# GpSimd's instruction order in the first pass of branch B, written by hand

## The chip, the cores and the metric

The kernel runs on one core of a Trainium2 chip. The core has a matrix engine (TensorE, PE in the views, with PEld for its weight loads), VectorE (DVE), ScalarE (ACT), GpSimd (POOL) and SyncE (SP), which here only issues DMAs. Each engine takes its instructions strictly in the order in which they stand in its stream, and semaphores hold an instruction until what it needs is there. The metric is the device time of one execution in microseconds (us), lower is better.

## The reference

One encoder block over 1024 tokens and 16 meta tokens, width 1024. Cut to what matters here:

```python
h = concat(meta, x)                       # 1040 x 1024
proj = rms_norm(h) @ w_in                 # qa ka va | qb kb vb | ga gb
y_a = differential_attention(qa, ka, va)  # branch A: 4 heads, two softmaxes each, all keys
y_b = windowed_gqa(qb, kb, vb, sink)      # branch B: 8 heads in 2 groups, band of 3 blocks + meta
merged = sigmoid(ga) * (y_a @ w_ba) + sigmoid(gb) * (y_b @ w_bb)
h = h + merged @ w_o
h = h + swiglu(rms_norm(h), w_gate, w_up, w_down)
out = rms_norm(h)[16:]

# branch B, for a block of 128 queries
p = exp(s - m)                            # s: scores + bias, m: their maximum and the sink's
denom = sum(p) + exp(sink - m)
y = (p / denom) @ v
```

Matrix products are done with operands split in a high and a low part (high = the value rounded to the matrix engine's fp32r format, low = the rest), so that one product is three: high x high, high x low, low x high.

## The kernel before

**Stages.** The normed input is transposed into `hT_hi` and `hT_lo`. The first projections (kb, and the queries of group 0 of branch B) run while it is still being transposed. Then comes the stretch of the program that the change touches: `attend_b` for the first two tiles of branch B, the projection vb (`project_v(C_VB, ...)`, L503), the other six tiles of group 0 (`units_b(0, qb, first_b)`, L646), the projections qa, va, ka of branch A's heads 0 and 1 (`project_a(0)`, `project_a(1)`), and, in four chunks, the token sums (`token_sums(c)`, L510). After it come the queries of group 1 (`project_qb(1, qb)`), the tiles of group 1 together with heads 2 and 3, then branch A's attention with the gates, the merge, and the feed-forward layer. The token sums are differences and sums of quarters of `hT` for products in Strassen's manner; they are stored in `ts_d` and read again only by `load_sums`, first at L706, after all projections.

**One tile of branch B** (`attend_b`, L316): for each of 4 heads two matmuls make scores in a PSUM bank (`bps`, L331, two banks), VectorE adds the bias and takes the running minimum of the negated scores into the SBUF tile `bs` (L333, two buffers), ScalarE takes exp with the row sum (L337), VectorE adds the sink's term and takes the reciprocal (`bdn`, L340 and L341), GpSimd scales the four heads' rows by it (L343) and copies the meta columns into `bmd` (L347). `finish` transposes each block on TensorE (`bpt`, L356, two PSUM banks), ScalarE writes the high part and VectorE the low part (`btr`, L358 and L360), TensorE multiplies with `vb` (`bpy`, L362, one bank), and `by` goes to DRAM. A middle tile has four blocks, an end tile three.

**One projection** is three chunks of tokens (two for qa and qb) by 8 weight blocks by 3 terms, L214. `prep` (L174) loads a weight tile `w_c`, ScalarE writes its high part `wh_c` and GpSimd (for most) the low part `wl_c` by a subtraction (`split`, L118). The third of the three terms needs `wl_c`. The names carry the weight's column: c2176 is vb, c0 / c1024 / c512 are qa, va, ka of head 0, c128 / c1152 / c640 those of head 1.

**One chunk of token sums** is 11 additions or subtractions of 128x512 on GpSimd into `ta` tiles (three buffers), four of whose results `keep` splits on ScalarE and VectorE into `to` (two buffers) and stores.

**What sets the order.** Up to branch A's attention a scheduler orders the instructions of every engine: it simulates the program on a timeline and takes what is ready there, so that the program's text is only a preference. GpSimd alone is ordered by hand (`tc.manual_schedule(engines={Pool})`: as the text has it) from L682 on, just ahead of the queries of group 1. TensorE is ordered by hand from branch A's attention on.

Of the kernel before, what the change touches and what calls it, by code (L numbers as in the profile page):

```python
# [73 lines left out]
def encoder_block(ctx: ExitStack, tc: tile.TileContext, x, meta, norm_mix, w_in, lq1, lk1, lq2, lk2,  # L74
# [7 lines left out]
    def f32(ap):  # L82
        return ap.bitcast(F32)
# [32 lines left out]
    def split(hi, lo, src, lo_eng):  # L116
        nc.scalar.activation(hi, src, AF.Copy)  # L117
        lo_eng.tensor_tensor(lo, src, f32(hi), ALU.subtract)  # L118
# [55 lines left out]
    def prep(col, name, p=None, lo_eng=None):  # L174
        w = wpool.tile([P, DC, P], F32, tag="w", name=f"w_{name}", bufs=2)
        if isinstance(col, tuple):
            for i, k in enumerate(col):
                nc.sync.dma_start(w[:, 4 * i:4 * i + 4], g_weights(k, 1, 0, P))
        else:
            nc.sync.dma_start(w, w_in[:, col:col + P].rearrange("(c p) n -> p c n", p=P))  # L180
        if p:
            both = p.tile([P, 2, DC, P], F32R, tag="k0", name=f"wb_{name}", bufs=1)
            wh, wl = both[:, 0], both[:, 1]
        else:
            wh = wpool.tile([P, DC, P], F32R, tag="wh", name=f"wh_{name}", bufs=W_BUFS)
            wl = wpool.tile([P, DC, P], F32R, tag="wl", name=f"wl_{name}", bufs=W_BUFS)
        split(wh, wl, w, lo_eng or nc.gpsimd)
        return wh, wl
# [11 lines left out]
    def ensure(n):  # L200
        while order and len(prepped) < n:
            col = order.pop(0)
            prepped[col] = prep(col, f"c{col[0] if isinstance(col, tuple) else col}", lo_eng=nc.vector if col in on_vector else None)
# [3 lines left out]
    def project_steps(col, chunks, name, evac):  # L207
        wh, wl = prepped.pop(col)
        terms = [(wh, hT_hi), (wh, hT_lo), (wl, hT_hi)]
        for at, n in chunks:  # L210
            ps = pp_bank(f"pp_{name}_{at}")
            for c in range(DC):
                for i, (a, b) in enumerate(terms):
                    nc.tensor.matmul(ps[:, :n], a[:, c, :], b[:, c, at:at + n],  # L214
                                     start=(c == 0 and i == 0), stop=(c == DC - 1 and i == 2))
                if c == DC - 1:
                    evac(ps[:, :n], at, n)
                yield

    def project(col, chunks, name, evac):  # L220
        ensure(1)
        for i, _ in enumerate(project_steps(col, chunks, name, evac)):
            if i % DC == V_AT and turning_v:
                next(turning_v[0], None)
        ensure(W_BUFS - 1)

    def evac_split(scale, consume):
        def run(ps, at, n):
            st = stage.tile([P, 2, 512], F32R, tag="qk", name="qk_stage", bufs=QK_BUFS)
            hi, lo = st[:, 0, :n], st[:, 1, :n]  # L230
            if scale is None:
                nc.scalar.activation(hi, ps, AF.Copy)
                nc.vector.tensor_tensor(lo, ps, f32(hi), ALU.subtract)
            else:
                nc.scalar.activation(hi, ps, AF.Copy, scale=scale)
                nc.vector.scalar_tensor_tensor(lo, ps, scale, f32(hi), ALU.mult, ALU.subtract)
            consume(f32(st), at, n)
        return run

    def project_v(col, name, evac):  # L240
        vt = vtpool.tile([P, L + NM], F32, tag="vt", name=f"vt_{name}", bufs=1)
        project(col, K_CHUNKS, name, lambda ps, at, n: nc.scalar.copy(vt[:, at:at + n], ps))
        nc.vector.tensor_copy(vt[:, L:L + NM], vt[:, S:L])

        def turn():
            for b in range(3):
                nb = 4 if b < 2 else 1
                kp = P if b < 2 else 2 * NM
                pt = pp_bank(f"pv_{name}_{b}").rearrange("p (c t) -> p c t", c=4)
                for i in range(nb):  # L250
                    k = 4 * b + i
                    nc.tensor.transpose(pt[:kp, i, :], vt[:, k * P:k * P + kp], ident)
                evac(pt[:kp, :nb, :], 4 * b, nb, kp)
                yield

        turning_v[:] = [turn()]
# [39 lines left out]
    def new_qb(g):  # L296
        return bpool.tile([P, 4, S], F32R, tag="qb", name=f"qb{g}", bufs=1)
# [73 lines left out]
    qb = new_qb(0)  # L371
# [127 lines left out]
    nc.vector.tensor_scalar(neglam, lam_s[:, 1:2], lam_s[:, 0:1], LAMBDA_INIT, ALU.subtract, ALU.subtract)  # L499


    first_b = [attend_b(0, t, qb) for t in range(2)]
    project_v(C_VB, "vb", vb_evac)  # L503
    flush_v()
    def quad(hl, kh, half):
        return (hT_hi, hT_lo)[hl][:, 4 * kh:4 * kh + 4, half * 512:half * 512 + 512]
# [3 lines left out]
    def token_sums(c):  # L510
        tt = nc.gpsimd.tensor_tensor

        def new(name):
            return tpool.tile([P, 512], F32, tag="ta", name=f"ta{name}_{c}", bufs=3)

        def part(hl, kh, half):
            return f32(quad(hl, kh, half)[:, c])

        def keep(p, src):
            to = tpool.tile([P, 2, 512], F32R, tag="to", name=f"to{p}_{c}", bufs=2)  # L520
            split(to[:, 0], to[:, 1], src, nc.vector)
            nc.sync.dma_start(ts_d[p][:, :, c, :], f32(to))

        t1, low = new(1), new("l1")
        tt(t1, part(0, 0, 1), part(0, 0, 0), ALU.subtract)
        tt(low, part(1, 0, 1), part(1, 0, 0), ALU.subtract)
        tt(t1, t1, low, ALU.add)
        keep(5, t1)
        t3, t2 = new(3), new(2)
        tt(t3, part(0, 1, 1), part(0, 0, 1), ALU.subtract)  # L530
        tt(t2, part(1, 1, 1), part(1, 0, 1), ALU.subtract)
        tt(t3, t3, t2, ALU.add)
        keep(7, t3)
        tt(t2, t3, part(0, 0, 0), ALU.add)
        tt(t2, t2, part(1, 0, 0), ALU.add)
        keep(6, t2)
        t4 = new(4)
        tt(t4, part(0, 1, 0), t2, ALU.subtract)
        tt(t4, t4, part(1, 1, 0), ALU.add)
        keep(4, t4)  # L540

    def project_a(h):
        def q_consume(st, at, n):
            for m in range(2):
                nc.sync.dma_start(qa_d[h][m, :, at:at + n].rearrange("(a d) t -> d a t", a=2),
                                  st[64 * m:64 * m + 64, :, :n])

        def k_consume(st, at, n):
            for m in range(2):
                nc.sync.dma_start(ka_d[h][m, :, at:at + n].rearrange("(a d) t -> d a t", a=2),  # L550
                                  st[64 * m:64 * m + 64, :, :n])

        def va_evac(pt, k0, nb, kp):
            vs = stage.tile([P, 2, 4, P], F32R, tag="qk", name="va_stage", bufs=QK_BUFS)
            hi, lo = vs[:kp, 0, :nb, :], vs[:kp, 1, :nb, :]
            nc.scalar.activation(hi, pt, AF.Copy)
            nc.vector.tensor_tensor(lo, pt, f32(hi), ALU.subtract)
            nc.sync.dma_start(va_d[h][:kp, :, k0:k0 + nb, :], f32(vs)[:kp, :, :nb, :])

        project(C_QA + h * P, Q_CHUNKS, f"qa{h}", evac_split(-(2.0 ** (2 * h - 1)), q_consume))  # L560
        project_v(C_VA + h * P, f"va{h}", va_evac)
        project(C_KA + h * P, K_CHUNKS if h < AH - 1 else K_CHUNKS[::-1], f"ka{h}", evac_split(None, k_consume))

    def units_b(g, qb, pending=(), extra=lambda t: None):
        pending = list(pending)
        for t in range(len(pending), NT):
            if len(pending) > 1:
                pending.pop(0)()
            pending.append(attend_b(g, t, qb))
            extra(t)  # L570
            if len(pending) > 1:
                pending.pop(0)()
        for p in pending:
            p()
# [68 lines left out]
                what(g_done[i])  # L643
                g_done[i] += 1

    units_b(0, qb, first_b)  # L646
    for c in range(2):
        token_sums(c)
    project_a(0)
    token_sums(2)  # L650
    project_a(1)
    token_sums(3)

    def load_k(h, m, k):
        nc.sync.dma_start(f32(k)[:, 0, :], ka_d[h][m])
# [23 lines left out]
        nc.sync.dma_start(f32(v)[2 * NM:3 * NM, 0, 8, :], va_d[h][:NM, 1, 8, :])  # L679
        return v  # L680

    order_pool = tc.manual_schedule(engines={mybir.EngineType.Pool})  # L682
    order_pool.__enter__()
    qb = new_qb(1)
    project_qb(1, qb)
    for n in range(2):
# [210 lines left out]
    for n in range(AH * NT + T_LAG):  # L897
        scoring, turning = iter(()), iter(())
        if n < AH * NT:
            h, t = divmod(n, NT)  # L900
# [548 lines left out]
    for n in range(nf, len(steps)):  # L1449
# [4 lines left out]
        if p in LOADS:  # L1454
            at, half, col = LOADS[p]
            if at <= j < at + 4:
                t, cols = 4 * half + j - at, slice(col * 512, col * 512 + 512)
# [60 lines left out]
```

## Time and profile before

| | us |
|---|---|
| median of 3 runs | 1446.95 (1446.73 to 1448.22) |
| the profiled execution | 1446.43 |
| its span, first to last instruction | 1444.6 |

| engine | busy us | share of the span | instructions |
|---|---|---|---|
| TensorE matmuls | 1423.5 | 99% | 7279 |
| TensorE weight loads | 1221.1 | 85% | 7279 |
| VectorE | 901.6 | 62% | 1624 |
| ScalarE | 679.5 | 47% | 1290 |
| GpSimd | 642.6 | 44% | 605 |

The profile is one execution. Matmuls are pipelined: a record lasts until its end, which is modelled, and the next one starts earlier. So what a matmul costs in a dense stream is the step from one start to the next, and "busy" does not mean that TensorE ran at its peak. Times in the views are counted from the span's start. Of the 1444.6 us, the stretch that the change touches lies between about 35 us (the first token sum on GpSimd in the kernel before) and 200 us (the first score of group 1).

### The profile page before, as it was taken

The page shows a single profiled execution, that of the slowest core. Times are in us where ns is not written, and L with a number is a line of the kernel's source. Part 1 is how long each engine was busy: PE and PEld are TensorE (multiplying, and loading weights), DVE is VectorE, ACT ScalarE, POOL GpSimd, SP SyncE. Part 2 cuts the span into 40 slices and gives each one's busy share as a digit, 9 for nine tenths or more (in the row PEclk, how much of TensorE's full clock was granted, in tenths as well). Part 3 has the DMA queues.
Part 4 walks back from the last instruction along what each step waited for, and adds up shares of the span by engine and source line. Part 5 has one row for each costly group of instructions (what it writes and reads, how often), then busy time and mean ns, then how long its engine had stood idle before and what let it go on. Part 6 is the DMA issues. An engine that isn't in the chain of part 4 may idle for free.

```text
span 1444.6 us, 21159 instructions
## 1 busy us (share of the span) xinstructions
PE 1423.5 (99%) x7279; PEld 1221.1 (85%) x7279; DVE 901.6 (62%) x1624; ACT 679.5 (47%) x1290; POOL 642.6 (44%) x605
## 2 busy tenths in 40 slices
PE   8999999999999999999999999999999999999997
PEld 6988989988898989888888878888888888888886
DVE  7478536637697989624614966554555553787567
ACT  6356535545665656545413643333333333444454
POOL 5589227743333333334522665544544552000444
PEclk9999999999999999999999999999999999999999
DMA  8367668995558473586602534333332333964343
GB/s 245 87 211 231 195 160 271 283 289 208 189 168 258 147 226 126 190 255 204 224 32 88 152 103 162 110 102 110 101 103 96 110 102 102 334 205 140 124 130 139
DMA packets 188891, 242.41 MB, mean 168 GB/s; under 512 B 18208, under 2 KB 115936, under 8 KB 188784
## 3 DMA queue, kind: packets, MB, share of 16 engines
q1 hardware_dynamic: 188784, 241.07, 52.5%
q8 instruction: 57, 0.93, 0.3%
q14 instruction: 50, 0.41, 0.1%
HBM read 157.45 MB, written 77.00 MB: 162 GB/s over the span
## 4 chain that ended last, share of the span: by engine, by line
PE 80%; POOL 6%; DVE 5%; issue 4%; DMA 3%; ACT 2%; SPq 0%; POOLq 0%; DVEq 0%; ACTq 0%
PE pg L1299 27%; PE pd L1393 9%; PE pg L742 7%; PE ppa L786 6%; PE po L1076 6%; PE aps L802 3%; PE pp_qb L214 3%; PE apy L841 3%; POOL oa L118 3%; PE pp_ka L214 2%; PE pp_va L214 2%; PE apt L828 2%; PE pp_qa L214 2%; PE bpt L356 1%; PE bpy L362 1%
## 5 line engine op out<-in xcount | busy, mean ns | idle before, releaser
L118 POOL TENSOR_TENSOR wop<-wf,wop 128x512 fp32r<-128x512 f32 x128 | 173.5, 1360 | 164.7 <-ACT wop L117 150.3
L1299 PE MATMUL pg<-t,wop 128*128 128x512 f32 x1056 | 242.6, 389 | 0.0
L1299 PEld LDWEIGHTS pg<-t,wop 128*128 128x128 f32 x1056 | 198.2, 188 | 41.2
L1393 PE MATMUL pd<-ob,oa 128*128 128x512 f32 x924 | 209.9, 389 | 0.4 <-POOL oa L118 0.4
L1393 PEld LDWEIGHTS pd<-ob,oa 128*128 128x128 f32 x924 | 173.3, 188 | 36.8 <-POOL oa L118 0.9
L1299 PE MATMUL pg<-b,wop 128*128 128x512 f32 x792 | 185.6, 392 | 2.3 <-DVE c L1308 2.3
L1299 PEld LDWEIGHTS pg<-b,wop 128*128 128x128 f32 x792 | 149.4, 189 | 34.2 <-issue 2.4
L742 PE MATMUL pg<-hT_hi,gop 128*128 128x512 f32 x384 | 142.9, 397 | 0.0
L118 POOL TENSOR_TENSOR oa<-ra,oa 128x512 fp32r<-128x512 f32 x33 | 44.1, 1337 | 170.0 <-ACT oa L117 168.6
L117 ACT ACTIVATE wop<-wf 128x512 fp32r<-128x512 f32 x128 | 80.2, 631 | 83.3 <-PE pg L1299 47.8
L118 POOL TENSOR_TENSOR gop<-gr,gop 128x512 fp32r<-128x512 f32 x47 | 62.0, 1321 | 105.9 <-ACT gop L117 105.9
L117 ACT ACTIVATE oa<-ra 128x512 fp32r<-128x512 f32 x77 | 48.7, 632 | 106.1 <-PE pd L1393 46.0
L810 ACT ACTIVATE as<-as,amn 128x1040 f32<-128x1040 f32 x64 | 74.5, 1165 | 47.3 <-DVE amn L805 43.2
L1134 DVE TENSOR_TENSOR s<-wf,wf 128x512 f32<-128x512 f32 x22 | 23.7, 1077 | 107.6 <-DMA wf<-in_w_ff_gate_dram 57.4
L802 PE MATMUL aps<-ak,aq 128*128 128x392 f32 (+1 forms) x384 | 90.1, 330 | 0.7 <-DVE amn L805 0.4
L1076 PE MATMUL po<-woh,mT 128*128 128x512 f32 x384 | 88.1, 390 | 0.0
L1076 PEld LDWEIGHTS po<-woh,mT 128*128 128x128 f32 x384 | 71.9, 188 | 14.8
L742 PEld LDWEIGHTS pg<-hT_hi,gop 128*128 128x128 f32 x384 | 72.7, 189 | 11.3 <-DVE gk L747 0.2
L802 PEld LDWEIGHTS aps<-ak,aq 128*128 128x128 f32 x384 | 69.6, 189 | 14.3 <-DVE amn L805 2.0
L343 POOL TENSOR_SCALAR bs<-bs,bdn 128x432 f32<-128x432 f32 (+1 forms) x64 | 41.1, 662 | 87.1 <-DVE bdn L341 74.3
L742 PE MATMUL pg<-hT_lo,gop 128*128 128x512 f32 x192 | 76.1, 396 | 0.0
L813 POOL TENSOR_SCALAR as<-as,adn,neglam 128x1040 f32<-128x1040 f32 x32 | 39.1, 1220 | 63.9 <-DVE adn L811 44.6
(289 smaller groups left out, 3105.9 us busy)
## 6 DMA issues: line engine op xcount, KB each, us to landing
ra<-aop SPq DMA_DIRECT2D x77, 256.0 KB, 2.7
wf<-in_w_ff_gate_dram SPq DMA_DIRECT2D x24, 512.0 KB, 3.8
wf<-in_w_ff_up_dram SPq DMA_DIRECT2D x24, 512.0 KB, 3.9
aop<-as SPq DMA_DIRECT2D x44, 256.0 KB, 2.1
w_c<-in_w_in_dram SPq DMA_DIRECT2D x17, 512.0 KB, 6.1
aop<-c SPq DMA_DIRECT2D x33, 256.0 KB, 2.0
ts_d<-to SPq DMA_DIRECT2D x16, 512.0 KB, 3.4
gw<-in_w_in_dram SPq DMA_DIRECT2D x32, 256.0 KB, 4.2
```

Of the source, the lines that this page charges most:

```text
L117: nc.scalar.activation(hi, src, AF.Copy)
L118: lo_eng.tensor_tensor(lo, src, f32(hi), ALU.subtract)
L214: nc.tensor.matmul(ps[:, :n], a[:, c, :], b[:, c, at:at + n], start=(c == 0 and i == 0), stop=(c == DC - 1 and i == 2))
L343: nc.gpsimd.tensor_scalar(st[:, r, :W], st[:, r, :W], dn[:, r:r + 1], 1.0, ALU.mult, ALU.mult)
L742: nc.tensor.matmul(ps, op[:, a, c], quad(b, *act)[:, c], start=(p in (2, 5, 1) and c == 0 and i == 0), stop=(p in (2, 3, 4) and c == 3 and ...
L786: nc.tensor.matmul(ps, w[:, a, j, :], src(j, b, tk), start=(j == 0 and n == 0), stop=(j == 3 and n == 2))
L802: nc.tensor.matmul(ps[:, :n], qs[m][:, t * P:(t + 1) * P], ks[m][:, vv, k0:k0 + n], start=(vv == 0), stop=(vv == 1))
L810: nc.scalar.activation(s[m][:, 0:L], s[m][:, 0:L], AF.Exp, bias=low, scale=-1.0, accum_out=dn[:, m:m + 1])
L841: nc.tensor.matmul(py[:, cols], v[:kp, a, k, :], at_[:kp, k, b, :], start=(k == 0 and j == 0), stop=(k == 8))
L1076: nc.tensor.matmul(ps, mT[:, c, a, t * P:(t + 1) * P], wos[q, c][:, b], start=(c == 0 and n == 0), stop=(c == DC - 1 and n == 2))
L1299: nc.tensor.matmul(ps, op[:, x, c, :], b[:, y, c, :], start=(p in (1, 2, 5) and c == 0 and n == 0), stop=(p in (4, 2, 3) and c == 3 and n ...
L1393: nc.tensor.matmul(ps[u], oa[:, a, u * P:(u + 1) * P], ob[:, b, :], start=(p in (1, 2, 5) and j == 0 and k == 0), stop=(p in (2, 3, 4) and ...
```

## The change

```diff
@@ project
                 next(turning_v[0], None)
         ensure(W_BUFS - 1)
+        step_sums(6)
+
+    summing = []
+
+    def step_sums(n):
+        while n > 0 and summing:
+            n -= 1
+            if next(summing[0], True):
+                summing.pop(0)
@@ ahead of branch B's first tile
+    order_pool = tc.manual_schedule(engines={mybir.EngineType.Pool})
+    order_pool.__enter__()
     first_b = [attend_b(0, t, qb) for t in range(2)]
     project_v(C_VB, "vb", vb_evac)
@@ token_sums: a yield behind each of the 11 operations
         tt(t1, part(0, 0, 1), part(0, 0, 0), ALU.subtract)
+        yield
         tt(low, part(1, 0, 1), part(1, 0, 0), ALU.subtract)
+        yield
...
@@ the order of the stages
-    units_b(0, qb, first_b)
-    for c in range(2):
-        token_sums(c)
+    summing += [token_sums(c) for c in range(4)]
+    units_b(0, qb, first_b, lambda t: step_sums(2))
     project_a(0)
-    token_sums(2)
     project_a(1)
-    token_sums(3)
+    step_sums(100)
@@ ahead of group 1
-    order_pool = tc.manual_schedule(engines={mybir.EngineType.Pool})
-    order_pool.__enter__()
     qb = new_qb(1)
```

GpSimd's order by hand now begins ahead of branch B's first tile. In it stand the scalings of the tiles, two token sums behind each of the tiles 2 to 7, and six behind each projection of heads 0 and 1. No operation is added or taken away. The other engines are still ordered by the scheduler, which now sees GpSimd's order as given; their streams differ from the kernel before up to the queries of group 1 and are the same, instruction for instruction, behind them.

GpSimd, from the last token sums of chunk 0 in the kernel before. `ta` are token sums, `wl_c2176` the low part of vb's weight, `bs_0_0` tile 0 of group 0:

```order
L539 TENSOR_TENSOR ta4_0_1607<-ta4_0_1607,hT_lo_134 128x512
L118 TENSOR_TENSOR wl_c2176_938<-w_c2176_935,wh_c2176_937 128x1024
L118 TENSOR_TENSOR wl_c0_1022<-w_c0_1019,wh_c0_1021 128x1024
L343 TENSOR_SCALAR bs_0_0_868<-bs_0_0_868,bdn_0_0_870 128x288 x4
L347 COPY bmd0_150<-bs_0_0_868 128x4x32
L526 TENSOR_TENSOR tal1_1_1615<-hT_lo_134 128x512
L343 TENSOR_SCALAR bs_0_1_901<-bs_0_1_901,bdn_0_1_903 128x432 x4
```

and in the changed kernel, from the same place of the program (behind the last of the input norms):

```order
L352 TENSOR_SCALAR bs_0_0_870<-bs_0_0_870,bdn_0_0_872 128x288 x4
L356 COPY bmd0_150<-bs_0_0_870 128x4x32
L352 TENSOR_SCALAR bs_0_1_903<-bs_0_1_903,bdn_0_1_905 128x432 x4
L356 COPY bmd1_151<-bs_0_1_903 128x4x32
L118 TENSOR_TENSOR wl_c2176_940<-w_c2176_937,wh_c2176_939 128x1024
L118 TENSOR_TENSOR wl_c0_1024<-w_c0_1021,wh_c0_1023 128x1024
L352 TENSOR_SCALAR bs_0_2_1089<-bs_0_2_1089,bdn_0_2_1091 128x432 x4
L356 COPY bmd0_150<-bs_0_2_1089 128x4x32
L536 TENSOR_TENSOR ta1_0_1122<-hT_hi_133 128x512
```

The two weight splits stood ahead of the first scaling and now stand behind the second; chunk 0 of the sums, which stood ahead of both, now begins behind the third.

TensorE at branch B's first tile before (`pp_vb` is the projection vb, `bps_0_0` the scores of tile 0):

```order
L214 MATMUL pp_vb_384_967<-hT_hi_133,wl_c2176_938 128x384
L214 MATMUL pp_vb_384_967<-hT_hi_133,wh_c2176_937 128x384
L214 MATMUL pp_vb_384_967<-hT_lo_134,wh_c2176_937 128x384
L214 MATMUL pp_vb_384_967<-hT_hi_133,wl_c2176_938 128x384
L331 MATMUL bps_0_0_0_872<-kb0_146,qb0_156 128x288
L331 MATMUL bps_0_0_1_876<-kb0_146,qb0_156 128x288
L214 MATMUL pp_vb_384_967<-hT_hi_133,wh_c2176_937 128x384
```

and in the changed kernel:

```order
L340 MATMUL bps_0_2_3_1105<-kb0_146,qb0_156 128x432 x2
L365 MATMUL bpt_0_0_8_1076<-ident_109,bmd0_150 128x128 x4
L365 MATMUL bpt_0_1_0_1127<-ident_109,bs_0_1_903 128x128 x2
L340 MATMUL bps_0_3_0_1174<-kb0_146,qb0_156 128x432 x2
L365 MATMUL bpt_0_1_0_1127<-ident_109,bs_0_1_903 128x128
L340 MATMUL bps_0_3_1_1178<-kb0_146,qb0_156 128x432 x2
L365 MATMUL bpt_0_1_0_1127<-ident_109,bs_0_1_903 128x128
L365 MATMUL bpt_0_1_1_1137<-ident_109,bs_0_1_903 128x128 x4
L365 MATMUL bpt_0_1_2_1147<-ident_109,bs_0_1_903 128x128 x4
L214 MATMUL pp_vb_0_943<-hT_hi_133,wl_c2176_940 128x384
```

Only the first six of vb's 72 matmuls (two terms of each of its three chunks) stood ahead of the scores of tile 0; the other 66 moved behind the scores and transposes of tiles 0 and 1 and scores of tiles 2 and 3.

TensorE among the later tiles before (`pp_ka0` is ka of head 0):

```order
L331 MATMUL bps_0_4_2_1253<-kb0_146,qb0_156 128x432 x2
L214 MATMUL pp_ka0_0_1797<-hT_hi_133,wl_c512_1793 128x384
L214 MATMUL pp_ka0_0_1797<-hT_hi_133,wh_c512_1792 128x384
L331 MATMUL bps_0_4_3_1257<-kb0_146,qb0_156 128x432 x2
L214 MATMUL pp_ka0_0_1797<-hT_lo_134,wh_c512_1792 128x384
L214 MATMUL pp_ka0_0_1797<-hT_hi_133,wl_c512_1793 128x384
L214 MATMUL pp_ka0_384_1836<-hT_hi_133,wh_c512_1792 128x384
L362 MATMUL bpy_0_2_1197<-btr_0_2_1_1203,vb0_148 128x512 x2
```

and in the changed kernel (`pp_va0` is va of head 0):

```order
L340 MATMUL bps_0_4_2_1267<-kb0_146,qb0_156 128x432 x2
L340 MATMUL bps_0_4_3_1271<-kb0_146,qb0_156 128x432 x2
L371 MATMUL bpy_0_2_1211<-btr_0_2_3_1237,vb0_148 128x512
L365 MATMUL bpt_0_3_2_1291<-ident_109,bs_0_3_1170 128x128 x4
L214 MATMUL pp_va0_768_1754<-hT_hi_133,wh_c1024_1681 128x272
L214 MATMUL pp_va0_768_1754<-hT_lo_134,wh_c1024_1681 128x272
L340 MATMUL bps_0_5_0_1338<-kb0_146,qb0_156 128x432 x2
L340 MATMUL bps_0_5_1_1342<-kb0_146,qb0_156 128x432 x2
L371 MATMUL bpy_0_2_1211<-btr_0_2_8_1247,vb0_148 128x512
L365 MATMUL bpt_0_3_3_1301<-ident_109,bs_0_3_1170 128x128 x4
```

Before, matmuls of projections stand between the tiles' own. Now these two of va are the last projection matmuls until tile 7's transposes: the third term of va needs `wl_c1024`, which in GpSimd's new order stands behind the scaling of tile 7 and one token sum. From there on ka, qa, va, ka of heads 0 and 1 and the queries of group 1 follow with no tile among them.

More of the change, by code (lines that the diff above doesn't have):

```diff
@@ L525, in token_sums @@
         tt(t1, part(0, 0, 1), part(0, 0, 0), ALU.subtract)
+        yield
         tt(low, part(1, 0, 1), part(1, 0, 0), ALU.subtract)
+        yield
         tt(t1, t1, low, ALU.add)
+        yield
         keep(5, t1)
@@ L530, in token_sums @@
         tt(t3, part(0, 1, 1), part(0, 0, 1), ALU.subtract)
+        yield
         tt(t2, part(1, 1, 1), part(1, 0, 1), ALU.subtract)
+        yield
         tt(t3, t3, t2, ALU.add)
+        yield
         keep(7, t3)
         tt(t2, t3, part(0, 0, 0), ALU.add)
+        yield
         tt(t2, t2, part(1, 0, 0), ALU.add)
+        yield
         keep(6, t2)
@@ L538, in token_sums @@
         tt(t4, part(0, 1, 0), t2, ALU.subtract)
+        yield
         tt(t4, t4, part(1, 1, 0), ALU.add)
+        yield
         keep(4, t4)
```

## The prediction

> **What bounds the kernel now.** I read the page's engine table first, then busy time by window, then TensorE's timeline.
>
> ```profile
> span 1444.6 us, 21159 instructions
> PE 1423.5 (99%) x7279; PEld 1221.1 (85%) x7279; DVE 901.6 (62%) x1624; ACT 679.5 (47%) x1290; POOL 642.6 (44%) x605
> ...
> core 0: us, PE busy (x) PEld busy (x) DVE busy (x) ACT busy (x) POOL busy (x), PEclk, DMA share, GB/s
> 56.04:200.53 144.49, 142.69 (x819) 128.85 (x818) 84.89 (x172) 72.80 (x168) 76.87 (x76) 1.00 0.67 193
> ```
>
> TensorE is the bound everywhere, and in the stretch that the change touches (from vb's first matmul to group 1's first score) it lacks only 144.49 - 142.69 = 1.8 us of being always busy. A GpSimd order can win little here; it can lose what it makes TensorE wait. Since "busy" hides short stalls, I price TensorE's work by steps from one start to the next:
>
> ```profile
> 56.04 0.34 PE L214 MATMUL pp_vb<-hT_hi,wh_c 128*128 128x384 f32 x1
> 56.22 0.34 PE L214 MATMUL pp_vb<-hT_lo,wh_c 128*128 128x384 f32 x1
> ...
> 63.39 0.43 PE L331 MATMUL bps<-kb,qb 128*128 128x288 f32 x2
> 63.65 0.34 PE L214 MATMUL pp_vb<-hT_hi,wh_c 128*128 128x384 f32 x1
> ...
> 65.22 0.29 PE L214 MATMUL pp_vb<-hT_hi,wl_c 128*128 128x272 f32 x1
> 65.34 0.29 PE L214 MATMUL pp_vb<-hT_hi,wh_c 128*128 128x272 f32 x1
> ...
> 73.26 0.40 PE L214 MATMUL pp_qa<-hT_hi,wh_c 128*128 128x512 f32 x1
> 73.49 0.40 PE L214 MATMUL pp_qa<-hT_lo,wh_c 128*128 128x512 f32 x1
> ...
> 89.70 0.55 PE L331 MATMUL bps<-kb,qb 128*128 128x432 f32 x2
> 90.09 0.34 PE L214 MATMUL pp_va<-hT_hi,wh_c 128*128 128x384 f32 x1
> ...
> 92.41 1.04 PE L356 MATMUL bpt<-ident,bs 128*128 128x128 f32 x8
> 93.20 0.42 PE L214 MATMUL pp_va<-hT_hi,wh_c 128*128 128x384 f32 x1
> ...
> 200.37 0.69 PE L331 MATMUL bps<-kb,qb 128*128 128x288 f32 x4
> ```
>
> A matmul of 384 columns takes 0.175 us, 512: 0.23 (512/384 x 0.175 = 0.233), 272: 0.12, 432: 0.39/2 = 0.195, 288: 0.26/2 = 0.13, a transpose 0.79/8 = 0.10. The same instructions lie between 56.04 and 200.37 in both kernels, 144.3 us, and the streams behind are equal, so what this stretch gains or loses is the whole result.
>
> **The change, part by part. First gap: vb waits for two scalings.** Before, vb covered tile 0's latency. Now TensorE runs 6 of vb's matmuls and stands before tile 0's scores, which need keys that SP's queue is still sending:
>
> ```profile
> 60.01 0.61 SPq L285 DMA_DIRECT2D kb<-qk_stage  x1
> ...
> DMA to landing us min/median/max: 2.0/2.1/3.8
> ```
>
> This is the last issue for group 0; it lands at 60.01 + 2.1 = 62.1. The queue holds the same DMAs in the same order, so nothing comes sooner. The chain behind it:
>
> ```profile
> 65.03 0.52 DVE L333 CUSTOM_DVE_ANT_0 bs<-bps,tbx,nsink 128x288 f32<-128x288 f32 x1 [7.28 <-PE bps L331]
> ...
> 82.36 1.29 POOL L527 TENSOR_TENSOR ta<-ta,tal 128x512 f32<-128x512 f32 x1
> 83.62 2.40 POOL L118 TENSOR_TENSOR wl_c<-w_c,wh_c 128x1024 fp32r<-128x1024 f32 x1
> ...
> 90.79 2.45 POOL L343 TENSOR_SCALAR bs<-bs,bdn 128x432 f32<-128x432 f32 x4 [1.56 <-ACT btr L358]
> ...
> 156.32 0.08 DVE L333 DVE_READ_ACCUMULATOR2_ANT bmn<- 128x1 f32 x1
> ...
> 157.84 1.96 POOL L343 TENSOR_SCALAR bs<-bs,bdn 128x288 f32<-128x288 f32 x4 [5.85 <-ACT btr L358]
> 159.87 0.29 POOL L347 COPY bmd<-bs 128x128 f32<-128x128 f32 x1
> ```
>
> From 62.1: score and hand-over 0.6, four minima of 0.55: 64.9. From a tile's last minimum to its scaling 157.84 - 156.40 = 1.44, and 0.7 for minima of tile 1 that stand between: 67.0. Scaling 1.96 and transposes 0.4: 69.4. In VectorE's new stream two minima of tile 2 stand ahead of tile 1's reciprocal and need the buffer that these transposes free: two of 0.73 (minimum plus its read, rows below), reciprocal and hand-over 0.3: 71.2. Tile 1's scaling 2.45, copy 0.29, `wl_c2176` 2.40, hand-over 0.2: vb's third matmul term starts at 76.5. TensorE's work till then: 6 of vb 0.9, scores 8 x 0.13 + 20 x 0.195 = 4.9, 24 transposes 2.4, together 8.3 of 20.5 us. **12 us idle.**
>
> **Middle, dense.** Rest of vb 10.3 (44 x 0.175 + 22 x 0.12), its transposes 0.9, 8 scores 1.6, qa 48 x 0.233 = 11.2, 20 transposes 2.0, 17 `bpy` 4.0, four of va 0.7, about 1.0 for vb's eviction: 31.6, to 108.1.
>
> **Second gap: tiles 4 to 7 alone.** Until `wl_c1024`, behind tile 7's scaling, only 2 projection matmuls remain. The tiles then go at their own period. VectorE carries most per tile:
>
> ```profile
> L118 DVE TENSOR_TENSOR to<-ta,to 128x512 fp32r<-128x512 f32 x10 | 11.2, 1121 | 7.4 <-ACT to L117 7.2
> L333 DVE CUSTOM_DVE_ANT_0 bs<-bps,tbx,nsink 128x432 f32<-128x432 f32 x14 | 8.7, 656 | 0.9 <-PE bpt L356 0.9
> L360 DVE TENSOR_TENSOR btr<-bpt,btr 128x512 fp32r<-128x512 f32 x13 | 8.4, 673 | 0.0
> L340 DVE TENSOR_TENSOR bdn<-bdn,bes 128x4 f32<-128x4 f32 x5 | 4.8, 968 | 0.9 <-ACT bes L339 0.9
> L335 DVE TENSOR_TENSOR bes<-bmn,sinkb 128x4 f32<-128x4 f32 x5 | 3.5, 707 | 0.1
> L366 DVE TENSOR_TENSOR by<-bpy,by 64x512 f32<-64x512 f32 x4 | 2.7, 674 | 1.2 <-ACT by L365 1.2
> L333 DVE DVE_READ_ACCUMULATOR2_ANT bmn<- 128x1 f32 x18 | 1.4, 78 | 0.0
> ```
>
> Four minima 4 x 0.734 = 2.9, four low parts 2.7, `by` 0.7: 6.3. The two four-column operations and one `to` add 2.8 at these means, 9.1 in all; but 0.7 to 1.0 us for four columns is mostly waiting, beside five or six sums and a split per tile on GpSimd, where now two sums stand. Half of the 2.8 gives 7.7; 0.5 for hand-overs: **8.2 us per tile.** Bounds: GpSimd's own work, 2.45 + 0.29 + 2 x 1.29 = 5.3, below; above, the spacing of two scalings in group 1, 231.49 - 220.61 = 10.9:
>
> ```profile
> 220.61 2.44 POOL L343 TENSOR_SCALAR bs<-bs,bdn 128x432 f32<-128x432 f32 x4 [2.41 <-DVE bdn L341]
> ...
> 231.49 3.49 POOL L343 TENSOR_SCALAR bs<-bs,bdn 128x432 f32<-128x432 f32 x4 [0.95 <-PE pp_va L214]
> ```
>
> From 108.1: two scores 0.8, two minima 1.5, 1.4 to the scaling, a low part 0.7 between: tile 4 scales at 112.5. Three periods 24.6, then scaling 1.96, copy 0.29, sum 1.29, split 2.40 = 5.9: va resumes at 143.0. TensorE's work in these 35 us: 28 scores 4.9, 72 transposes 7.2, 30 `bpy` 7.0, 0.2 of va = 19.3. **15.6 us idle.**
>
> **Rest, dense.** va 10.3, tile 7's rest 1.6, three of 72 narrow matmuls (48 x 0.175 + 24 x 0.12 = 11.3) 33.8, qa 11.2, va's transposes 1.8, group 1's queries 96 x 0.233 = 22.4: 81.1, to 224.1. Before: 200.4. **+23.7.**
>
> **Check of the ledger.** Its work is 8.3 + 30.6 + 19.3 + 81.1 = 139.3 for 144.3 us before; 1.8 of the 5.0 missing is idle, 3.2 is rounding and stalls of interleaving. Half of that (1.3, its share in the dense parts) I add: +25.0.
>
> **The moved sums** cost nothing: after 143.0 GpSimd has 32 sums and 4 splits, 41 + 10 = 51 us, under 81 us of projections. Their 16 stores pass SP's queue in that time too, and their ScalarE and VectorE halves find both engines free of tiles. Between two splits stand at most six sums, 6 x 1.29 + 2.40 = 10.1, against 11.2 of a projection; were that cover gone, about 1 us per projection, four times.
>
> **The clock.** An idle TensorE is followed by half clock here:
>
> ```profile
> 832.00:834.00 2.00, 0.17 (x1) 0.21 (x2) 2.00 (x4) 0.24 (x1) 1.99 (x1) 1.00 0.10 33
> 834.00:836.00 2.00, 2.00 (x7) 1.56 (x7) 2.00 (x4) 0.87 (x2) 0.22 (x1) 0.64 0.03 8
> 836.00:838.00 2.00, 2.00 (x6) 1.55 (x5) 2.00 (x4) 0.14 (x1) 0.00 (x0) 0.51 0.00 0
> ...
> 833.83 6.43 PE L1299 MATMUL pg<-b,wop 128*128 128x512 f32 x20 [2.01 <-DVE c L1308]
> ```
>
> After 2.01 us without a matmul the granted clock is 0.64 and 0.51 of two windows: (0.36 + 0.49) x 2 / 0.5 = 3.4 us at half, 1.7 us lost. Both gaps end in dense work; bounds 0 to 3.4, I take 1.7. **+26.7: 1446.43 + 26.7 = 1473.** (This execution is 0.5 below the median, which I leave.)
>
> The Trainium skill, "TensorE: Matmul & The Clock Gate" (Part 1, What's actually happening; Part 4), lets the clock fall after an idle window of about 3.4 us and says that transposes do not count as busy in the same way. The trace agrees on the 3.4 us at half but has it fall after 2.0 us of idleness. By that page the clock could stay low through the whole second gap, which is the third case below.
>
> **The rivals.** *GpSimd-bound tiles*: the short GpSimd queue lets tiles run at 5.3, VectorE's small operations at nothing. 3 x 2.9 = 8.7 less: **1464**. Against it: 6.3 us of VectorE alone. *Slow clock*: at half clock the 19.3 us of the second gap's work become 38.6, more than the gap, so TensorE bounds the tiles; with the 10.9 period 3 x 2.7 = 8.1 more: **1481**. For it: the idle share, 15.6 of 35; against: a busy window restores the clock. *Not slower*: scaling early lets VectorE and TensorE start each tile sooner, and vb is not held, if `wl_c2176` were done before 57. That needs both scalings before 57, while their keys land at 62.1, so it fails by 5 us at its first step; its price is at best the 1.8 us of idle time (or 3 with the hidden stalls): **1443 to 1445**.
>
> **How the numbers follow.** Forecast (period 7 to 10) 0.63; GpSimd-bound 0.16; slow clock 0.15; not slower 0.06, half of it within 0.2%, which is about what a measurement tells from no change. Faster 0.03, same 0.03, slower 0.94. Range: the low case less a first gap 1.5 shorter and no clock loss (1464 - 3 = 1461); the high case with the clock's other 1.7 and 1 in the sums (1484).
>
> **What would show it.** In the changed profile: a TensorE wait from about 57 to 62 ended by a DMA or by scores; vb's third term released by GpSimd's split near 76; scalings of tiles 4 to 7 some 8 us apart; va resuming near 143 behind `wl_c1024`; group 1's first score near 225 to 227; PEclk below 1.00 in both gaps; and all later stages shifted, not changed. Wrong would be: vb running before 70, tiles 5 us apart, or a later stage that gives time back.

## The result: 1480.8 us, and the profile after

| | before | after |
|---|---|---|
| median us (lowest to highest) | 1447.59 (1446.73 to 1448.81) | 1480.77 (1480.11 to 1483.31) |
| ratio, 95% interval | | 1.0231 [1.0218, 1.0243] |
| profiled execution, us | 1446.43 | 1480.49 |
| group 1's first score, us from the start | 200.37 | 232.54 |

The forecast was 1473 us, range 1461 to 1484. The change costs 33 us by the medians and 34.1 between the two profiled executions; of these, 32.2 are lost before group 1's first score, where the prediction looked for them. (One execution among the experiments, of e10, took 2466 us at a granted clock of 0.64 and is left out of every number below.) Busy time of the changed kernel by window, cut at the points that the prediction named:

```profile
core 0: us, PE busy (x) PEld busy (x) DVE busy (x) ACT busy (x) POOL busy (x), PEclk, DMA share, GB/s
56.00:62.00 6.00, 2.00 (x10) 1.31 (x10) 0.48 (x1) 0.47 (x1) 0.00 (x0) 1.00 0.43 76
62.00:70.00 8.00, 7.38 (x26) 5.23 (x25) 5.50 (x21) 5.42 (x18) 2.25 (x5) 0.57 0.42 83
70.00:78.50 8.50, 4.82 (x27) 3.11 (x26) 7.22 (x16) 4.80 (x13) 6.44 (x7) 1.00 0.11 27
78.50:108.00 29.50, 29.43 (x152) 25.55 (x151) 9.11 (x26) 10.88 (x28) 11.37 (x15) 0.94 0.20 60
108.00:144.20 36.20, 29.19 (x157) 21.09 (x155) 31.44 (x74) 28.06 (x67) 22.60 (x29) 1.00 0.30 89
144.20:232.50 88.30, 84.36 (x453) 77.35 (x454) 31.12 (x38) 25.20 (x44) 50.01 (x33) 0.96 0.78 243
```

Rows one to three are the first gap (TensorE works 14.2 of 22.5 us, part of it at a clock of 0.57), row five the second (29.2 of 36.2). A busy record lasts until its modelled end, so these are not the 8.3 and 19.3 us of work that the prediction counted by steps. The surprise is the last row: the part that I had down as dense took 88.3 us instead of 81.1, with 3.9 us idle and a clock of 0.96. GpSimd's timeline has the scalings of tiles 0, 1 and 4 to 7 and the two splits that end the gaps; the PE rows show what ended the wait each time (start, duration, idle time before it in brackets):

```profile
67.10 1.96 POOL L352 TENSOR_SCALAR bs<-bs,bdn 128x288 f32<-128x288 f32 x4 [35.87 <-DVE bdn L350]
71.84 2.42 POOL L352 TENSOR_SCALAR bs<-bs,bdn 128x432 f32<-128x432 f32 x4 [2.43 <-ACT bs L346]
74.77 4.67 POOL L118 TENSOR_TENSOR wl_c<-w_c,wh_c 128x1024 fp32r<-128x1024 f32 x2 [0.16 <-PE bps L340]
...
115.99 2.43 POOL L352 TENSOR_SCALAR bs<-bs,bdn 128x432 f32<-128x432 f32 x4 [11.85 <-ACT by L374]
124.17 2.68 POOL L352 TENSOR_SCALAR bs<-bs,bdn 128x432 f32<-128x432 f32 x4 [2.78 <-DVE bdn L350]
131.72 2.68 POOL L352 TENSOR_SCALAR bs<-bs,bdn 128x432 f32<-128x432 f32 x4 [1.91 <-DVE bdn L350]
137.76 2.43 POOL L352 TENSOR_SCALAR bs<-bs,bdn 128x288 f32<-128x288 f32 x4 [0.43 <-ACT by L374]
141.77 2.36 POOL L118 TENSOR_TENSOR wl_c<-w_c,wh_c 128x1024 fp32r<-128x1024 f32 x1
```

```profile
60.48 0.51 PE L340 MATMUL bps<-kb,qb 128*128 128x288 f32 x2 [2.47 <-issue]
61.83 0.56 PE L340 MATMUL bps<-kb,qb 128*128 128x288 f32 x2 [0.84 <-DMA kb<-qk_stage]
...
77.98 0.66 PE L365 MATMUL bpt<-ident,bs 128*128 128x128 f32 x4 [2.69 <-DVE btr L369]
78.39 0.42 PE L214 MATMUL pp_vb<-hT_hi,wl_c 128*128 128x384 f32 x1
...
144.18 0.44 PE L214 MATMUL pp_va<-hT_hi,wl_c 128*128 128x384 f32 x1 [0.69 <-POOL wl_c L118]
...
197.08 1.12 PE L261 MATMUL pv_va<-ident,vt_va 128*128 128x128 f32 x4 [3.94 <-ACT vt_va L251]
...
232.54 0.69 PE L340 MATMUL bps<-kb,qb 128*128 128x288 f32 x4
```

The first two gaps have the forecast's places. The wait at 197.08 is new. ScalarE's timeline says why:

```profile
186.41 0.46 ACT L251 COPY vt_va<-pp_va 128x384 f32<-128x384 f32 x1
196.03 0.63 ACT L117 ACTIVATE to<-ta 128x512 fp32r<-128x512 f32 x1 [9.16 <-DMA ts_d<-to]
196.57 0.46 ACT L251 COPY vt_va<-pp_va 128x384 f32<-128x384 f32 x1
```

`to` has two buffers. The high part of a token sum (L117) waits 9.2 us on ScalarE until an earlier sum's store has landed; the copy of va (L251) that TensorE needs stands behind it in ScalarE's order. The store that it waits for went out at 185.84 and is the slowest of the 12 in this part to land, 10.1 us later (SP's timeline, then the landing times of these stores):

```profile
185.84 0.56 SPq L533 DMA_DIRECT2D ts_d<-to  x1
DMA to landing us min/median/max: 3.0/4.6/10.1
```

### The profile page after: what moved, and what is told of

It is laid out like the page before. It is cut to its first block, busy times and chain, and to the rows that moved or that the text cites. A ratio compares the mean times of both kernels' runs of the same rounds, so it can differ in the third digit from the quotient of the medians.

```text
span 1478.7 us, 21173 instructions
## 1 busy us (share of the span) xinstructions
PE 1435.9 (97%) x7279; PEld 1223.5 (83%) x7279; DVE 897.4 (61%) x1624; ACT 680.7 (46%) x1290; POOL 637.5 (43%) x605
## 4 chain that ended last, share of the span: by engine, by line
PE 76%; POOL 6%; issue 5%; DMA 5%; DVE 4%; ACT 3%; SPq 1%; POOLq 0%; ACTq 0%; DVEq 0%
PE pg L1316 26%; PE pd L1410 9%; PE pg L759 6%; PE ppa L803 6%; PE po L1093 6%; PE aps L819 3%; POOL oa L118 3%; PE apy L858 3%; PE pp_ka L214 2%; PE pp_qb L214 2%; PE pp_qa L214 2%; PE apt L845 2%; PE pp_va L214 2%; PE bps L340 1%; PE bpt L365 1%
## 5 line engine op out<-in xcount | busy, mean ns | idle before, releaser
L117 ACT ACTIVATE wop<-wf 128x512 fp32r<-128x512 f32 x128 | 80.2, 631 | 83.8 <-PE pg L1316 47.5
L117 ACT ACTIVATE oa<-ra 128x512 fp32r<-128x512 f32 x77 | 48.7, 632 | 105.7 <-PE pd L1410 43.9
```

## The experiments

Each is the changed kernel with one or two edits, timed against the kernel before on the same chip. "va" is the start of its third term, "dense" the time from there to group 1's first score (both read from TensorE's timeline).

| run | median us | ratio, 95% | va | first score | dense |
|---|---|---|---|---|---|
| changed kernel | 1480.77 | 1.0231 [1.0218, 1.0243] | 144.18 | 232.54 | 88.4 |
| e1 splits first | 1463.58 | 1.0106 [1.0091, 1.0121] | 133.82 | 215.58 | 81.8 |
| e2 va's split early | 1483.38 | 1.0246 [1.0228, 1.0263] | | 235.87 | |
| e4 both mended | 1448.62 | 1.0008 [0.9999, 1.0018] | | 196.95 | |
| e6 sums early | 1482.50 | 1.0231 [1.0214, 1.0248] | 151.97 | 238.58 | 86.6 |
| e10 heads only | 1468.88 (three) | 1.0151 [1.0134, 1.0169] | | | |
| e10b the same again | 1467.02 (one) | | | 217.78 | |
| e8 late keys | 1481.24 | 1.0235 [1.0218, 1.0253] | 145.00 | 235.65 | 90.7 |
| e7 no sums among | 1473.77 | 1.0175 [1.0150, 1.0199] | 141.38 | 226.21 | 84.8 |
| e9 sums after group 1 | 1523.40 | 1.0534 [1.0513, 1.0555] | 142.46 | 224.34 | 81.9 |
| e11 both mended, sums late | 1446.93 | 1.0006 [0.9997, 1.0016] | | 196.52 | |

**e1, splits first.** The first gap alone is mended.

```
     order_pool.__enter__()
+    ensure(2)
     first_b = [attend_b(0, t, qb) for t in range(2)]
```

> The weight splits of vb and of head 0's queries are put ahead of branch B's first scaling again; all else is as in the changed kernel. Theory (each gap is a projection whose split stands behind tiles in GpSimd's order): vb runs at once from 56, the first gap of some 12 us and the half clock behind it are gone; the cover is then used up earlier, and tiles 3 to 7 run alone at 7 to 8 us each: tile 0 scales near 69, tile 7 near 69 + 7 x 8 = 125, va goes on near 131 instead of 144.1: 1480.8 - 12 = 1466 to 1471. Rival (the tiles' chain from tile 0 at 67 sets when tile 7 ends, whatever covers it, so the first gap's gain is paid in the second): va goes on within 3 us of 144: 1477 to 1482.

Measured: 1463.6, below the theory's range. Busy time of two stretches by window (columns as above):

```profile
86.00:134.00 48.00, 39.88 (x209) 29.45 (x208) 41.50 (x99) 37.23 (x91) 33.19 (x43) 0.96 0.24 73
133.80:215.60 81.80, 81.78 (x450) 74.85 (x451) 32.14 (x38) 25.30 (x45) 51.46 (x33) 1.00 0.85 262
```

va goes on 10.4 us sooner (144.18 - 133.82), where the theory had some 13 (near 131); TensorE is still idle 8.1 of 48 us where tiles 3 to 7 run alone. The other 6.6 us come from the dense part: 81.8 us, never idle, clock 1.00. Nothing in the edit touches that part. So the 81.1 of the forecast were right as work, and what the changed kernel loses there is a stall that can be absent with all its sums in place.

**e2, va's split early**, to give the second gap a cover.

```
-    units_b(0, qb, first_b, lambda t: step_sums(2))
+    units_b(0, qb, first_b, lambda t: (step_sums(2), ensure(2 if t == 2 else 1)))
```

> The split that releases the third term of head 0's values is put behind tile 2 instead of behind tile 7; the first gap stays. Theory: the second gap gets va's 66 matmuls (10.3 us of TensorE work) as its cover, group 1's first score comes some 10 us sooner (232.7 to 223): 1468 to 1473, less 1.7 if the half clock behind the gap goes too. Rival (the tiles' chain is lengthened by as much as it is covered, because VectorE and ScalarE must also evict va among the tiles): 1478 to 1482.

Measured: 1483.4, above both ranges. The theory fell; of the rival, that the tiles' chain gets longer came true, but more was lost in another way. GpSimd's timeline, then a row of TensorE's:

```profile
149.96 1.95 POOL L352 TENSOR_SCALAR bs<-bs,bdn 128x288 f32<-128x288 f32 x4
151.97 0.65 POOL L356 COPY bmd<-bs 128x128 f32<-128x128 f32 x1
152.58 1.29 POOL L536 TENSOR_TENSOR ta<-hT_hi 128x512 f32<-128x512 f32 x1
...
161.93 2.79 POOL L118 TENSOR_TENSOR wl_c<-w_c,wh_c 128x1024 fp32r<-128x1024 f32 x1
```

```profile
164.78 0.69 PE L214 MATMUL pp_ka<-hT_hi,wl_c 128*128 128x384 f32 x1 [7.88 <-POOL wl_c L118]
```

The old place is covered (TensorE works 37.25 of the 38 us from 108 to 146), but its tiles now take turns with va and tile 7 scales 12.2 us later (149.96 against 137.76). Then the next projection, ka, stands before its own split: seven sums lie ahead of it on GpSimd. The gap was handed to the next projection. This prices a sentence of the prediction: a batch of six sums without its cover was to cost "about 1 us per projection"; here seven cost 7.9 at once, since no dense projection was running above them.

**e4, both mended.** e1's edit, and `project_a` made a generator that yields behind its first two projections:

```
+    heads = chain(project_a(0), project_a(1))
+    units_b(0, qb, first_b, lambda t: (step_sums(2), next(heads, None)))
+    for _ in heads:
+        pass
-    units_b(0, qb, first_b, lambda t: step_sums(2))
-    project_a(0)
-    project_a(1)
```

> GpSimd's order is still by hand from branch B's first tile on, with two sums per tile and six per projection, but vb's split stands ahead of the first scaling and one projection of heads 0 and 1 stands behind each of tiles 2 to 7. Theory (not the hand, and not the sums, but the place of the splits costs the time): both gaps go, TensorE lacks under 5 us between 56 and group 1's first score, which comes at 200 to 208: 1445 to 1455. Rival (an order that GpSimd cannot leave makes TensorE wait wherever it is put, since sums and scalings stand in fixed turns): first score after 215, 1463 or more.

Measured: 1448.6, as the theory had it, not to be told from before. The whole stretch in one window:

```profile
56.00:196.90 140.90, 139.80 (x798) 125.77 (x797) 79.88 (x169) 71.39 (x164) 92.43 (x86) 1.00 0.61 182
```

TensorE lacks 1.1 us. The order is still by hand and has the same number of sums behind each tile and each projection; the place of the splits, and of the projections behind them, makes the whole difference. The first score at 196.95 is no gain on the 200.37 of before: 8 products and 12 transposes of group 0 that stood ahead of it there stand behind it here, some 3 us by the prediction's steps.

**e10, heads only**, e4 without e1's line: the second gap alone is mended.

> The changed kernel with one projection of heads 0 and 1 behind each of tiles 2 to 7, and vb's split left behind two scalings: the second gap alone is mended, as the run with the splits first mended the first alone. Theory (the two gaps add up, each is priced by its own cover): the first gap's 12 us and 1.7 of clock stay, so it stands that far above the run with both mended, 1448.6 + 13.7 = 1462, range 1459 to 1466; vb goes on near 77. Rival (the second gap follows from the first, because late tiles push everything behind them): 1470 or more, with TensorE still lacking over 10 us between 110 and 150.

Measured: 1468.9, above the theory's range and just under the rival's. The same kernel once more, for its trace:

> The same kernel as the run with heads 0 and 1 behind the tiles and vb's split left behind two scalings, once more for a trace, since the profiled execution of that run had a clock of 0.64 throughout. The timed ones gave 1469 to 1470, 21 above the kernel with both gaps mended, where my price of the first gap is 13.7. Theory (the first gap is longer than its idle time before vb: VectorE and the tiles behind it are late too, which the second gap hid in the changed kernel): vb goes on at 77 to 79, a further 5 to 8 us are lost between 79 and 200, at waits for VectorE or for a transfer. Rival (the first gap itself is 20 us here): vb goes on at 84 or later.

Measured: 1467.0. TensorE's timeline around vb, then those windows of 10 us that are shortest of work or clock:

```profile
79.94 0.66 PE L365 MATMUL bpt<-ident,bs 128*128 128x128 f32 x4 [2.69 <-DVE btr L369]
80.35 0.42 PE L214 MATMUL pp_vb<-hT_hi,wl_c 128*128 128x384 f32 x1
```

```profile
60.00:70.00 10.00, 7.25 (x20) 5.05 (x21) 4.92 (x19) 4.49 (x15) 1.52 (x4) 0.56 0.43 79
70.00:80.00 10.00, 6.33 (x31) 4.28 (x30) 7.80 (x20) 5.73 (x18) 6.71 (x9) 0.92 0.14 34
...
90.00:100.00 10.00, 8.55 (x38) 6.58 (x37) 7.82 (x17) 6.67 (x18) 7.57 (x6) 0.83 0.18 52
...
140.00:150.00 10.00, 7.66 (x44) 6.34 (x43) 7.73 (x15) 6.41 (x15) 9.78 (x9) 1.00 0.75 208
```

vb goes on at 80.4, between the two expectations, and about 5 us more go later: (10 - 8.55) + 1.7 of clock at 90 to 100, 2.3 idle at 140 to 150 (the rival had over 10 between 110 and 150). As a difference of whole runs, the first gap is worth 17.2 us (changed kernel less e1, but 6.6 of these lie in the dense part) or 18 to 20 (e10 and e10b less e4), not 13.7; the second 15.0 (e1 less e4) or 12 to 14 (changed kernel less e10 or e10b). The two prices don't add up exactly.

**e6, sums early**, four behind each tile (`step_sums(2)` becomes `step_sums(4)`), to clear the dense part of stores.

> Four sums instead of two behind each of tiles 2 to 7; the other 16 follow behind projections as before. It is to tell why the dense part behind the second gap took 88.6 us instead of 81.1. Theory (the token sums' stores stand in SP's queue beside the loads of the keys near 180 and land late, ScalarE stands before a sum and TensorE behind it): most stores are out before 170, ScalarE's waits before sums and the half clock at 195 to 202 go, 3.9 + 3.4 = 7.3 less; the tiles' period goes from 7.1 to at most 2.45 + 0.29 + 4 x 1.29 = 7.9, which gives up to 2.4 back: 1473 to 1477. Rival (the keys' loads are late for everyone and the sums have no part in it): 1480 to 1484.

Measured: 1482.5, the rival's number. Tile 7 scales 4.3 us later (142.07), va goes on 7.8 later, and the stall is there again under another name: group 1's queries on TensorE wait 3.7 us for an eviction of ka, whose staging buffer (the SBUF tile in which evicted values wait for their store) a late store of va holds. So the rival's cause, that the sums have no part in it, is not shown by this run; e9 speaks against it.

**e8, late keys.** GpSimd clears a column of head 0's key tiles behind the last sum, so that their loads go out late.

```
     def load_k(h, m, k):
+        if h == 0:
+            nc.gpsimd.memset(f32(k)[:, :, 0:1], 0.0)
```

> The changed kernel, but head 0's key tiles are first cleared in one column by GpSimd behind its last token sum, so that the six loads of these keys go out behind the sums' stores (near 195) instead of among them (177 to 185). Theory (the stores land late because these 260 to 520 KB loads go through the same 16 DMA engines at that moment; ScalarE stands before a sum and TensorE behind it): stores land in under 6 us, TensorE's 3.9 us before the transposes of va at 196 and the half clock behind it go, 1480.8 - 7.3 = 1473, range 1471 to 1476. Rival (the stall only moves to the next transfer or next user, as when the sums were put earlier): 1479 to 1484.

Measured: 1481.2; the rival again. The table of waits, of TensorE first, then of ScalarE (total us, times, longest):

```profile
PE pp_qb L214 <- DVE qk_stage L242: 6.5, 1, 6.5
```

```profile
ACT qk_stage L241 <- DMA va_d<-va_stage: 16.6, 3, 9.2
```

The keys' loads went out from 197.1 on, and the sums no longer stop TensorE; now va's stores land late, and ka's eviction waits for the staging buffer that they hold. So the late transfer is not one culprit: the wait falls on another buffer, again in a stretch that transfers fill (the DMA share was 1.02 and 1.04 from 200 to 220).

**e9, sums after group 1.** All sums behind group 1's tiles (`summing += ...` moved ahead of `project_a(2)`, `step_sums(100)` behind `project_a(3)`, none among the tiles).

> All 40 token sums are put behind group 1's tiles, so none of them and none of their stores is left in the dense part between the second gap and group 1's first score. The readout is this dense part (va's third term to the first score of group 1): 81.1 us were forecast, 88.4 were measured in the changed kernel, 81.8 with the splits first, 86.6 with four sums per tile, 90.7 with the keys' loads late, 85.6 with no sums among the tiles. Theory (the sums' traffic and their halves on ScalarE fill the part, and some user of a late transfer stops TensorE, another one each time): 81 to 82.5 us, no TensorE wait over 1 us, no half clock. Rival (the other transfers and the order of the projections do it without the sums): 85 or more, with a wait of 3 us or more again. The whole time is no test: 52 us of sums now stand before the gate products that read them, 1470 if something covers them, up to 1520 if nothing does.

Measured in the dense part: 81.9 us, the theory's value (for e7 the expectation says 85.6; by the row of va's third term it is 84.8). By window:

```profile
142.40:224.30 81.90, 81.90 (x456) 75.14 (x455) 18.44 (x26) 19.61 (x33) 8.85 (x4) 1.00 0.60 172
```

No idle time, full clock, DMA share 0.60 instead of 0.78, and VectorE at 18.4 us instead of 31.1. So without sums in this part the stall is gone. The whole, 1523.4, was to be lost, up to 1520 by the expectation: TensorE waits once 47.6 us at the first gate product for a split behind the sums.

**e7, no sums among the tiles** (the extra call of `units_b` left out).

> No token sums among the tiles; all 40 follow behind projections, six at a time. It is to tell what sets the tiles' period where they run alone (scalings of tiles 4 to 7 stood 8.2, 7.6 and 6.0 us apart). Theory (VectorE and the hand-overs set it, GpSimd's two sums per tile are hidden): the same spacings within 0.5, tile 7 scales at 136 to 138.5, va goes on 1 to 2 us sooner than 144.1 because one sum less stands ahead of its split; 1478 to 1484 with the twelve sums done later. Rival (the sums hold GpSimd and VectorE among the tiles): spacings of 5.3 to 6.3, tile 7 near 133, va near 138: 1472 to 1476.

Measured: 1473.8 in all, the rival's number, but half of it by luck: tile 7's scaling and va's third term (141.38) lie between the two expectations, 2.8 of the 7.0 us are gained up to va, and 3.5 in the dense part, of which the rival said nothing. (The token sums number 44, four chunks of 11, not 40.) The scalings of tiles 4 to 7 stand 7.9, 5.4 and 5.6 us apart, two of three in the rival's range:

```profile
117.10 2.44 POOL L352 TENSOR_SCALAR bs<-bs,bdn 128x432 f32<-128x432 f32 x4 [14.34 <-ACT by L374]
...
124.96 2.43 POOL L352 TENSOR_SCALAR bs<-bs,bdn 128x432 f32<-128x432 f32 x4 [5.07 <-DVE bdn L350]
...
130.39 2.43 POOL L352 TENSOR_SCALAR bs<-bs,bdn 128x432 f32<-128x432 f32 x4 [2.65 <-ACT by L374]
...
135.97 1.95 POOL L352 TENSOR_SCALAR bs<-bs,bdn 128x288 f32<-128x288 f32 x4 [2.80 <-ACT btr L367]
```

Of tile 5 the timelines show GpSimd's two sums in the changed kernel, beside them VectorE's operation on four columns for the sink, and the same operation in e7:

```profile
118.74 1.28 POOL L546 TENSOR_TENSOR ta<-hT_lo 128x512 f32<-128x512 f32 x1
120.10 1.29 POOL L548 TENSOR_TENSOR ta<-ta,ta 128x512 f32<-128x512 f32 x1
```

```profile
120.28 1.13 DVE L344 TENSOR_TENSOR bes<-bmn,sinkb 128x4 f32<-128x4 f32 x1
```

```profile
121.39 0.16 DVE L344 TENSOR_TENSOR bes<-bmn,sinkb 128x4 f32<-128x4 f32 x1
```

The same instruction takes 1.13 us beside a sum and 0.16 without one, and it ends at 121.41 when the sum does (121.39). So VectorE mostly sets the period, as the theory says (from tile 4's to tile 7's scaling it is busy 20.2 of 21.8 us in the changed kernel and 16.6 of 18.9 in e7), but the two sums per tile are not hidden: they add a low part of 0.66 on VectorE and hold up its small operations.

**e11, both mended, sums late**: e4 with `lambda t: next(heads, None)`, no sums among the tiles.

> The kernel with both gaps mended, but no sums behind the tiles: six behind each of the six projections, four at the end. Theory (sums are hidden under dense projections there, and the tiles no longer share GpSimd with two sums each): 1446 to 1449, not to be told from before. Rival (more sums late crowd the transfers before group 1, as in the dense part of the changed kernel): 1452 or more.

Measured: 1446.9, ratio 1.0006 [0.9997, 1.0016]: the theory. No version beat the kernel before; two are level with it.

## Why the prediction was right, and what was mis-sized

**TensorE bounds, little to win: right.** With both gaps mended the stretch is dense, and the whole is level with before, not faster.

**First gap: place and GpSimd's part in it right, the last release not; 1.9 us short.** Scalings at 67.10 and 71.84 (67.0 and 71.2 forecast), vb's third term at 78.39 (76.5). What ended the wait was not the split but VectorE: transposes of tile 1 stand before vb on TensorE and needed a `bpt` bank that VectorE's `btr` had yet to empty. VectorE was held by one four-column operation:

```profile
75.03 2.11 DVE L349 TENSOR_TENSOR bdn<-bdn,bes 128x4 f32<-128x4 f32 x1 [0.38 <-ACT bes L348]
```

It ends at 77.14, when the first of the two splits from 74.77 does (half of 4.67 later: 77.1). I had taken such excess for waiting beside GpSimd's sums and splits in the second gap, and allowed nothing for it in the first.

**Middle: right but for the clock.** Tile 4 scales at 115.99 instead of 112.5: 1.9 from above, and 1.8 of half clock behind 78.5 ((1 - 0.94) x 29.5).

**Second gap: right, a little too long.** Three periods take 21.8 us instead of 24.6; from tile 7's scaling to va 6.4 instead of 5.9. Period 7.3 for 8.2, within the bounds; e7 says why I was near: without sums a tile takes 6.3 us ((135.97 - 117.10) / 3, tile 4's to tile 7's scaling), and the sums add the rest. So va goes on at 144.18 for 143.0.

**The step that failed: "The moved sums cost nothing".** It counted GpSimd's 51 us under 81 us of projections and said that their stores, ScalarE and VectorE halves find room (16 stores by its count; 12 were left for this part). On average they do, and TensorE waits for no split there; but ScalarE takes sums and va's copies in one order, and a sum waits for a store. One such store landed 10.1 us after its issue, TensorE stood 3.9 us, and half clock followed. Of the 88.4 us, 3.9 are that wait, 2.6 the clock (84.36 busy against e1's 81.78), 0.7 the rest over 81.1. e9 shows that without sums the stall is gone, e6 and e8 that moving the sums or the keys' loads only changes its victim. But sums in this part don't suffice for it. In e1, with the same 12 stores, ScalarE waits for a store 0.8 us in the whole part (19.3 in the changed kernel), though one of them takes 9.0 us to land. In e7, with all 16 stores there, a sum waits 7.7 us for a store with va's copy behind it, and TensorE waits at most 1.1 us. What decides seems to be when the late store lands and what TensorE still has to do at that moment; why this fell badly in the changed kernel and well in e1 is open.

**Clock: the mechanism right, the size not.** I took 1.7 us in all, bounds 0 to 3.4. The two pieces on dense work alone are 1.8 and 2.6, together 4.4 and outside these bounds; the second follows the stall, not a gap. A third, at 0.57 from 62 to 70, lies in the first gap; what it costs there no run tells apart. The sign "PEclk below 1.00 in both gaps" failed for the second gap, where it stayed at 1.00.

**The ledger's correction of 1.3** was not needed: e1's and e9's dense parts, 81.8 and 81.9, are within 0.8 of the count.

**The sum.** Forecast 227.1 for group 1's first score. Measured: + 1.9 (vb) - 2.8 (periods) + 0.5 (tile 7 to va) + 7.2 (dense) - 1.3 (ledger) = 232.6; the half clock behind vb took the 1.7 that I had for both. That the time is within the range owes something to luck: the tiles' 2.8 us made up for part of the dense part's 7.2, and the range reached 1484 because of the slow-clock case, its remaining half clock and 1 us for the sums, not because a stall behind a store was foreseen. The other 1.9 us of the end come later, against "all later stages shifted, not changed": from the first score to the first product of `ppa` (the merge) the changed kernel takes 425.1 us, before 422.2, and 424.0 to 424.8 in e1, e7 and e8; about 1 us of it comes back by the end. The order there is the same; what it is stays open.

**Rivals.** *Slow clock* would have come out at the same 1481, and fell all the same: from 108 to 144 PEclk is 1.00, and the tiles ran at 7.3, not 10.9. By the Trainium skill, "TensorE: Matmul & The Clock Gate" (Part 4), transposes do not count as busy in the same way, so that the clock might have been low here. It was up with scores, transposes and `bpy` busy for 29 of 36 us. *GpSimd-bound tiles* fell: GpSimd is busy 22.6 of those 36 us. *Not slower* fell at its first step, the keys: a score waits for `kb` until 61.83.

## What to carry to other kernels

In an engine's order by hand, place first the instruction that feeds the bound engine. Ask for each wait of that engine how many instructions stand ahead of its releaser, and what dense work is left to run meanwhile. Mending one such place can hand the gap to the next projection, as in e2, unless its releaser moves too. Work "hidden" by the average is not hidden where another engine must take it in order behind a buffer that a late store holds.

## What the runs showed of the hardware

VectorE's four-column operations, with both inputs in SBUF, take 0.14 to 0.17 us alone, but 1.13 beside a sum and 2.11 beside a split, and each ends when GpSimd's operation does. The kernel before shows it too: between 100 and 135 us all six that begin beside a sum or a split take 0.97 to 2.32 us and end within 0.03 us of it. VectorE's score minima, with a PSUM operand, take 0.66 us beside the splits and elsewhere alike. The Trainium skill ("SBUF — State Buffer", Who interferes with whom) says that a VectorE instruction with two SBUF inputs contends with a GpSimd instruction that reads SBUF, and that the lock on the shared ports is exclusive. The runs agree, and my price for the sums among the tiles should have begun there.

Of the 512 KB stores, with a median of 4.6 us from issue to landing in the dense part, one took 10.1 beside other transfers (DMA share 1.06 from 180 to 190). TensorE's waits of 2.5 to 3.9 us in the changed kernel were each followed by half clock (0.57 from 62 to 70, 0.94 behind 78.5, 0.52 from 195 to 202), while one of 2.24 us at 148 in e10b was not (1.00 from 140 to 160).
